# FFN gate and up by seven block products for eight, with GpSimd sums of weight blocks

## The chip, the cores and the metric

The kernel runs on one core of a Trainium2 chip. The metric is device time in microseconds (us), the median over runs. A profile of one execution gives, for every instruction, when it ran on its engine and what it waited for. The engines are TensorE (PE; PEld is its weight load), VectorE (DVE), ScalarE (ACT), GpSimd (POOL) and SyncE (SP, which here issues the transfers). PSUM is the memory that TensorE writes its products to, SBUF the other memory on the chip.

## The reference

Two layers of a decoder trunk on 512 tokens with 1024 channels, in float32. Only the second half of a layer is changed, the gated feed-forward network (FFN):

```
h2 = rms_norm(x, g_ffn[l])                                  # x * 1/sqrt(mean(x*x) + eps) * g
gt = causal_dwconv(h2 @ w_ffn_gate[l], ffn_conv_w[l])       # 3 taps over tokens, by channel
x = x + (jax.nn.silu(gt) * (h2 @ w_ffn_up[l])) @ w_ffn_down[l]
```

The weights w_ffn_gate and w_ffn_up are 1024 x 2816 each, w_ffn_down is 2816 x 1024. The four mixing branches ahead of the FFN are left alone.

## The kernel before

Activations lie with channels on the 128 partitions and 512 tokens along a row. A float32 product is made of three passes: each operand is split into its rounding to float32r (hi) and the rest (lo), and hi*hi, hi*lo and lo*hi are added up in one PSUM bank. So every matmul has a 128x128 block of weights as its stationary operand and 512 tokens as the moving one, and three of them do one block of the product.

Weights come by SP in units of 512 KB (tile `raw`, four blocks of 128 rows by 256 columns), in the order of a list (`plan`). `split_weights` makes a unit's pair: ScalarE writes `hi` (line 283), VectorE writes `lo` as the difference (line 284). There are three buffers each of `hi` and `lo`, so the split of a unit starts when the unit three ahead of it in the list has been multiplied. `channels` multiplies two units for a pair of output tiles, and `tick` lets queued jobs emit work amid a unit. PE and VectorE run in the order in which the code is written; so does ScalarE by the program as built.

`feed` makes the operand of the FFN: for each of x's eight channel tiles k, `xh` and `xl` (lines 178, 179) and the sum of squares (lines 186, 187). The factor 1/sqrt(...) of the norm by token is not known yet when the first product begins. It is made by the job "rows": `columns` (four one-column matmuls over the summed squares, a root and a reciprocal), then `spread` (four transposes), which leaves it in `rows`.

`ffn` goes through the 22 tiles of 128 hidden channels in three parts (`PARTS`: 8, 8 and 6 tiles). In a part it takes two tiles at a time (a pair): gate's product (96 matmuls for gate and up together), times `rows` (line 981), the three taps (983, 986) and Silu (989) on VectorE and ScalarE; then up's product, the gate value times `rows` (994), times up (995), and its split into hi and lo (169, 170). Then `down` multiplies the part's tiles by w_ffn_down and adds the result to x (1006). In the last layer's last part down gives tokens on partitions, and `store` writes the output.

Of the kernel before, what the change touches and what calls it, by code (L numbers as in the profile page):

```python
# [23 lines left out]
P = 128  # L24
# [20 lines left out]
def turn_pieces(n=6, bits=11):  # L45
    """1 / (2 pi) as a sum of numbers of few bits."""
    from fractions import Fraction
    pi = Fraction(3141592653589793238462643383279502884197169399375105820974944592307816406286,
                  10 ** 75)
    rest, out = 1 / (2 * pi), []  # L50
    for _ in range(n):
        e = math.floor(math.log2(float(rest)))
        unit = Fraction(2) ** (e - bits + 1)
        piece = (rest // unit) * unit
        out.append(float(piece))
        rest -= piece
    return out
# [3 lines left out]
def trunk(ctx: ExitStack, tc, x, positions, g_mix, w_in, b_gate, g_qa, g_ka, g_kidx, w_oa,  # L61
# [18 lines left out]
    def b_tile():  # L80
        return tmp.tile([P, 542], F32, tag="b", name=nm("b"), bufs=6)

    def m5_tile(w=1280):
        return tmp.tile([P, w], F32, tag="m5", name=nm("m5"), bufs=3)

    def h8_tile(shape):
        return tmp.tile(shape, F32, tag="h8", name=nm("h8"), bufs=3)
# [19 lines left out]
    # ---------------------------------------------------------------- inputs  # L107
# [8 lines left out]
    # ---------------------------------------------------------------- vectors by channel  # L116
    # Their rows, turned to a column each.
# [35 lines left out]
    # ---------------------------------------------------------------- residual stream  # L153
# [13 lines left out]
    def split(hi, lo, src):  # L167
        """hi: src rounded to float32r; lo: the remainder (in place where lo is src)."""
# [3 lines left out]
    def feed(k, gname, l):  # L172
        """x's tile k as an operand, times its gain, and its squares; kept in DRAM while the
        branches need its place."""
        if gname == "g_mix" and k % 4 == 3:
# [4 lines left out]
                                       op1=OP.subtract)  # L180
        if k == 0:
# [6 lines left out]

    def inv_root(acc, n, rows, sums=None):
        """1 / sqrt(sum over channels / n + eps): by token, and that for all partitions in rows.  # L190
        Three stages, and where the first will be. sums: by token, in four parts each."""
# [25 lines left out]
    # ---------------------------------------------------------------- weights  # L217
    # In units (source, first k, k's, columns), in the order in which they are used.
# [13 lines left out]
    def ffn_units(w, l, f):  # L232
        return [(w[l, h * 512:(h + 1) * 512, f * P:(f + 2) * P], 4 * h, 4, 256) for h in range(2)]

    def down_units(l, f0, f1, p):
        h = (f1 - f0) // 2
        return [(w_ffn_down[l, (f0 + i * h) * P:(f0 + (i + 1) * h) * P, p * 256:(p + 1) * 256],
                 i * h, h, 256) for i in range(2)]

    def plan():  # L240
        for l in range(L):
# [20 lines left out]
            for f0, f1 in PARTS:  # L262
                for f in range(f0, f1, 2):
                    yield from ffn_units(w_ffn_gate, l, f)
                    yield from ffn_units(w_ffn_up, l, f)
                for p in range(4):
                    yield from down_units(l, f0, f1, p)

    def unit(tag, dtype, nk, w):
        t = wts.tile([P, UNIT], dtype, tag=tag, name=nm(tag), bufs=3)  # L270
        return t[:, :nk * w].rearrange("p (k n) -> p k n", k=nk)

    def fetch(src, nk, w):
        """[128 nk, w] of a matrix on chip, [128, nk, w]."""
        raw = unit("raw", F32, nk, w)
        nc.sync.dma_start(raw, src.rearrange("(k p) n -> p k n", p=P))  # L276
        return raw

    def split_weights(raw, nk, w, step):
        """The same as a pair of operands."""  # L280
# [9 lines left out]
    def fetch_next():  # L290
        u = stream.popleft()
        near.append((u, fetch(u[0], u[2], u[3])))

    def ahead(n, step=4):
        while len(ready) < n and (near or stream):
# [3 lines left out]
            ready.append((u, split_weights(raw, u[2], u[3], min(step, u[2]))))  # L299

    def weights(src, k0, nk, w):
        """The next pair of the plan; two more are under way."""
# [5 lines left out]
    # Work beside the products: jobs of stages, (cost on VectorE, what it does) each. A stage that  # L308
    # needs TensorE comes a tick after what it waits for.
# [16 lines left out]
    # late: the rest of a stage, once the others of its tick have begun.  # L326
# [85 lines left out]
    # ---------------------------------------------------------------- constants  # L412
# [9 lines left out]
    def make_constants():  # L422
        # [t, s]: 0 where s <= t, NEG elsewhere, in the last 128 columns.
# [3 lines left out]
        # [t, s]: 0 where s < t, NEG elsewhere.  # L427
# [19 lines left out]
    def make_angles(pos_i):  # L447
        """Cosines and sines of positions times frequencies; the rest of it as jobs."""
# [10 lines left out]
        def products():  # L459
# [8 lines left out]
            # The angle in turns: both factors in parts whose products are exact.  # L468
# [35 lines left out]
    def rope(v, nh, half, t, f0):  # L504
        """Rotates v [128 tokens, nh, width] by the angles of token tile t."""
# [13 lines left out]
    # ---------------------------------------------------------------- one layer's mixing  # L519
    def mixing(l, first):  # L520
# [5 lines left out]
        # Indexer queries, keys and weights, and the values, from x times gain; the norm after.  # L526
# [4 lines left out]
        def normed(ks):  # L531
            """The normed x takes the place of x times gain."""
# [32 lines left out]
        # --- indexer  # L565
# [62 lines left out]
        # --- attention queries and keys  # L628
# [25 lines left out]
        # --- selected attention, a head and 128 tokens at a time  # L654
# [69 lines left out]
        # --- conformer branch  # L724
        u, conv, yb = [], [], []

        def conv_taps(c, j0, j1):
            if j0 == 0:
                a = b_tile()
                nc.vector.tensor_scalar(a[:, :T], u[c][:, :T], col(f"cb_w{l}", c),  # L730
                                        col("cb_b", l * 4 + c), op0=OP.mult, op1=OP.add)
                conv.append(a)
# [55 lines left out]
        for p in range(2):  # L788
# [6 lines left out]
            ps = channels(in_units(l, O_GLU + 256 * p, 256), xop, 256)  # L795
            for c in range(2):
                a = b_tile()
# [14 lines left out]
        # --- short convolution branch  # L812
# [33 lines left out]
        def merge(n, y):  # L846
            """Adds a branch to the merged sum: its gate times its output projection."""
# [33 lines left out]
        # --- stick-breaking attention, keys in rows  # L881
# [16 lines left out]
        def stick(h, t):  # L898
# [3 lines left out]
            def weigh():  # L902
                """A key's weight: its break times the product of what later keys have kept."""
# [54 lines left out]
        for p in range(4):  # L958
            ps = channels(merge_units(l, p), merged, 256)
            for c in range(2):  # L960
                k = 2 * p + c
                nc.vector.tensor_tensor(xT[k], xT[k], ps[c], op=OP.add)
                feed(k, "g_ffn", l)

    # ---------------------------------------------------------------- one layer's FFN
    def ffn(l, last):
        done.clear()
        rows = act.tile([P, T], F32, tag="rows", name=nm("rows"), bufs=1)
        _, columns, invert, spread = inv_root(lambda: norm["acc"][:, :T], D, rows)
        job(0, "rows", [], PAUSE, (0.1, lambda: (columns(), invert())), (0.1, spread))  # L970
        budget[0], credit[0] = 0.1, 0.0
        for f0, f1 in PARTS:
            ops = []
            for f in range(f0, f1, 2):
                ps = channels(ffn_units(w_ffn_gate, l, f), xop, 256)
                need("rows")
                sl = []
                for c in range(2):
                    g = s_tile()
# [164 lines left out]
```

## Time and profile before

| | us |
|---|---|
| median of the timed runs | 1990.86 (1990.49 to 1990.98, 3 runs) |
| span of the profiled execution, first to last instruction | 1989.1 |
| PE busy in it | 1977.1 |
| DVE busy | 1314.1 |
| ACT busy | 777.7 |
| POOL busy | 11.8 |

The profiled execution has its span as its own time; the timed runs lie 1.8 us above it, which is what lies around the span. Busy times count an engine's running instructions; an engine that waits is idle. The granted clock is the share of TensorE's full clock of 2.4 GHz.

### The profile page before, as it was taken

How to read it: one execution, taken by the hardware profiler on the slowest of the kernel's cores; microseconds unless marked ns; L12 is line 12 of the kernel's file. 1: busy time of each engine (PE TensorE's matmuls, PEld its weight loads, DVE VectorE, ACT ScalarE, POOL GpSimd, SP SyncE). 2: the span in 40 equal slices, each digit the busy share in tenths (PEclk: the TensorE clock that was granted, in tenths of full speed). 3: DMA queues.
4: the chain of work that ended last, by engine and by line, in shares of the span. 5: the costliest groups of instructions: out<-in, count | busy, mean ns of one | idle time of the engine just before them, and what ended most of it. 6: DMA issues, size and time to landing. Idle time of an engine off the chain costs nothing.

```text
span 1989.1 us, 23980 instructions
## 1 busy us (share of the span) xinstructions
PE 1977.1 (99%) x9244; PEld 1642.2 (83%) x9244; DVE 1314.1 (66%) x2208; ACT 777.7 (39%) x1266; POOL 11.8 (1%) x129
## 2 busy tenths in 40 slices
PE   8999999999999999999999999999999999999999
PEld 7878888888888888888888888888888888888888
DVE  7887789767445654646667878896764556456364
ACT  6436442443634322222353464424444343223231
POOL 0000000000000000000000000000000000000000
PEclk9999999999999999999999999999999999999999
DMA  6333223233333333333342332232333323333322
GB/s 198 96 96 85 66 84 96 85 107 95 96 96 96 95 97 95 106 96 93 104 127 85 87 94 75 75 104 75 110 94 96 96 85 106 101 91 105 95 85 86
DMA packets 176440, 191.46 MB, mean 96 GB/s; under 512 B 6310, under 2 KB 167110, under 8 KB 175302
## 3 DMA queue, kind: packets, MB, share of 16 engines
q1 hardware_dynamic: 176326, 189.93, 31.8%
q8 instruction: 73, 1.20, 0.3%
q14 instruction: 41, 0.34, 0.1%
HBM read 183.62 MB, written 6.29 MB: 95 GB/s over the span
## 4 chain that ended last, share of the span: by engine, by line
PE 98%; DMA 1%; SPq 0%; ACT 0%; DVE 0%; issue 0%; ACTq 0%
PE mm L105 92%; PE at L105 4%; PE at L685 0%; PE at L927 0%; DMA x<-in_x_dram 0%; DMA raw<-in_w_in_dram 0%; PE at L650 0%; PE at L1022 0%; ACT hi L283 0%; SPq L435 0%; PE at L211 0%; PE at L589 0%; ACT L672 0%; SPq L125 0%; SPq L276 0%
## 5 line engine op out<-in xcount | busy, mean ns | idle before, releaser
L283 ACT ACTIVATE hi<-raw 128x1024 fp32r<-128x1024 f32 (+3 forms) x344 | 358.8, 1044 | 777.1 <-PE mm L105 730.2
L105 PE MATMUL mm<-xh,hi 128*128 128x512 f32 x1664 | 656.6, 395 | 0.0
L105 PE MATMUL mm<-xh,lo 128*128 128x512 f32 x1664 | 648.4, 390 | 0.0
L105 PE MATMUL mm<-xl,hi 128*128 128x512 f32 x1664 | 648.0, 389 | 0.0
L284 DVE TENSOR_TENSOR lo<-raw,hi 128x1024 fp32r<-128x1024 f32 (+2 forms) x342 | 412.2, 1206 | 320.1 <-ACT hi L283 320.1
L105 PE MATMUL mm<-q,hi 128*128 128x512 f32 x1248 | 396.9, 391 | 0.0
L105 PEld LDWEIGHTS mm<-xh,hi 128*128 128x128 f32 x1664 | 312.6, 188 | 67.9 <-issue 2.8
L105 PEld LDWEIGHTS mm<-xh,lo 128*128 128x128 f32 x1664 | 312.5, 188 | 65.5
L105 PEld LDWEIGHTS mm<-xl,hi 128*128 128x128 f32 x1664 | 312.7, 188 | 65.0 <-issue 1.0
L105 PEld LDWEIGHTS mm<-q,hi 128*128 128x128 f32 x1248 | 233.5, 188 | 49.8 <-issue 2.1
L105 PE MATMUL mm<-q,lo 128*128 128x512 f32 x688 | 268.0, 389 | 0.0
L736 DVE SCALAR_TENSOR_TENSOR b<-b,par,b 128x512 f32<-128x512 f32 x240 | 180.2, 751 | 6.9
L105 PEld LDWEIGHTS mm<-q,lo 128*128 128x128 f32 x688 | 129.2, 188 | 26.8
L105 PE MATMUL mm<-hi,xh 128*128 128x512 f32 (+1 forms) x320 | 120.3, 382 | 1.4 <-ACT hi L283 1.1
L105 PE MATMUL mm<-lo,xh 128*128 128x512 f32 (+1 forms) x320 | 117.9, 374 | 0.0
L105 PE MATMUL mm<-hi,xl 128*128 128x512 f32 (+1 forms) x320 | 117.9, 374 | 0.0
L169 ACT ACTIVATE q<-s 128x512 fp32r<-128x512 f32 x68 | 43.0, 632 | 98.6 <-DVE s L995 62.8
L105 PEld LDWEIGHTS mm<-hi,xh 128*128 128x128 f32 x320 | 60.6, 191 | 13.9 <-issue 1.9
L986 DVE SCALAR_TENSOR_TENSOR s<-s,par,s 128x512 f32<-128x512 f32 x88 | 66.2, 752 | 6.5 <-DVE s L983 0.5
L105 PEld LDWEIGHTS mm<-hi,xl 128*128 128x128 f32 x320 | 59.6, 188 | 10.1
L105 PEld LDWEIGHTS mm<-lo,xh 128*128 128x128 f32 x320 | 59.6, 188 | 9.7
L170 DVE TENSOR_TENSOR q<-s,q 128x512 fp32r<-128x512 f32 x52 | 36.0, 693 | 37.5 <-ACT q L169 37.5
(199 smaller groups left out, 1570.6 us busy)
## 6 DMA issues: line engine op xcount, KB each, us to landing
raw<-in_w_in_dram SPq DMA_DIRECT2D x152, 512.0 KB, 3.6
raw<-in_w_ffn_gate_dram SPq DMA_DIRECT2D x44, 512.0 KB, 3.7
raw<-in_w_ffn_up_dram SPq DMA_DIRECT2D x44, 512.0 KB
raw<-in_w_ffn_down_dram SPq DMA_DIRECT2D x32, 512.0 KB, 3.3
raw<-in_w_merge_dram SPq DMA_DIRECT2D x16, 512.0 KB, 4.0
raw<-in_w_ffn_down_dram SPq DMA_DIRECT2D x16, 384.0 KB, 2.9
away<-h SPq DMA_DIRECT2D x4, 1024.0 KB, 5.9
raw<-in_w_oc_dram SPq DMA_DIRECT2D x8, 512.0 KB, 3.4
```

The source lines that it names most:

```text
L105: return nc.tensor.matmul(*a, skip_group_check=True, **k)
L169: nc.scalar.activation(hi, src, AF.Copy)
L170: nc.vector.tensor_tensor(lo, src, hi.bitcast(F32), op=OP.subtract)
L283: nc.scalar.activation(hi[:, k:k + step], raw[:, k:k + step], AF.Copy)
L284: nc.vector.tensor_tensor(lo, raw, hi.bitcast(F32), op=OP.subtract)
L736: nc.vector.scalar_tensor_tensor(a[:, :T], u[c][:, j:j + T], col(f"cb_w{l}", j * 4 + c), a[:, :T], op0=OP.mult, op1=OP.add)
L986: nc.vector.scalar_tensor_tensor(a[:, :T], g[:, j:j + T], col(f"f_w{l}", 22 * j + f + c), a[:, :T], op0=OP.mult, op1=OP.add)
```

## The change

Gate and up of a pair form a matrix of 2 x 2 blocks: two halves of the input channels by (gate, up). With the tokens cut in two halves of H = 256, the product of such a pair takes eight block products, and Strassen's scheme (in Winograd's form) does it in seven, with sums of blocks of the weights and of the activations. A product is one `step`: 24 matmuls of 256 tokens, 168 for a pair.

* The sums of weight blocks are four GpSimd instructions over 128 x 1024 for each pair (`add` in `block`): s1 = up0 + up1, s2 = s1 + gate0, s3 = s2 - up1 (written over gate0), s4 = s2 + gate1. Each is then split by ScalarE and VectorE as a unit was.
* The sums of activation blocks are made by `feed_ffn`, in place of `feed`, once a layer.
* The sums of products are made in PSUM: a bank is copied (`after_g1`), or written by VectorE (`join`), and PE adds further products onto it.
* The norm's factor is no longer applied to the hidden values of up, but to down's result (lines 1217 and 1223); the first tap's product goes from VectorE to ScalarE, the small memset from GpSimd to VectorE.
* `quad_order` gives the order of the steps: g1 of the next pair comes ahead of s3, s4 and u2 of a pair; in a part's last pair the order is s1, s2, g2, s3, s4, u2.

```diff
+    def feed_ffn(k, l):
...
+        j = k - 4
+        e1, e2, d, d4 = s_tile(), s_tile(), s_tile(), s_tile()
+        nc.scalar.activation(e2[:, :T], xT[k], AF.Copy, scale=g)
+        nc.scalar.activation(e1[:, :T], xT[j], AF.Copy, scale=col("g_ffn", l * KD + j))
+        nc.scalar.activation(xh[k], xT[k], AF.Copy, scale=g)
+        t3, n2, t4 = d[:, :H], d[:, H:T], d4[:, :H]
+        nc.vector.tensor_tensor(t3, e2[:, H:T], e1[:, H:T], op=OP.subtract)
+        nc.vector.scalar_tensor_tensor(n2, t3, -1.0, e1[:, :H], op0=OP.mult, op1=OP.subtract)
+        nc.vector.scalar_tensor_tensor(t4, n2, -1.0, e2[:, :H], op0=OP.mult, op1=OP.subtract)
+        nc.vector.tensor_tensor(xl[k], e2[:, :T], xh[k].bitcast(F32), op=OP.subtract)
...
+        split(*both, d[:, :T])
+        split(*four, t4)
...
+        squared(k)
...
+    def quad_order(f0, f1):
+
+        yield f0, ("g1",)
+        for f in range(f0, f1, 2):
+            if f + 2 < f1:
+                yield f, ("s1", "g2", "s2")
+                yield f + 2, ("g1",)
+                yield f, ("s3", "s4", "u2")
+            else:
+                yield f, ("s1", "s2", "g2", "s3", "s4", "u2")
...
+        def add(to, x, what, op=OP.add):
+            nc.gpsimd.tensor_tensor(b[to], b[x], b[what], op=op)
...
+        if step == "s1":
+            load("s", w_ffn_up, 0, "raw", wts)
+            load("u2", w_ffn_up, 1, "b", tmp)
+            load("g2", w_ffn_gate, 1, "b", tmp)
+            add("s", "s", "u2")
+            return b["s"]
+        if step == "s2":
+            add("s", "s", "g1")
+            add("g1", "s", "u2", OP.subtract)
+            return b["s"]
+        if step == "s4":
+            add("s", "s", "g2")
+            return b["s"]
...
+    def product(l, f, step, bank, fresh):
+
+        hi, lo = block_weights(l, f, step)
+        for c in range(2):
+            dst = bank[:, c * H:(c + 1) * H]
+            for k in range(4):
+                oh, ol = comb[BLOCK_OF[step], k]
+                w = slice(c * P, (c + 1) * P)
+                mm(dst, hi[:, k, w], oh, start=fresh and c == k == 0, stop=False)
+                mm(dst, hi[:, k, w], ol, start=False, stop=False)
+                mm(dst, lo[:, k, w], oh, start=False, stop=k == 3)
+            if c == 0:
+                tick(budget[0])
...
+            def join():
+                v["z"] = ps_mm()
+                nc.vector.tensor_tensor(v["z"], v["v"], v["u"][:, :T], op=OP.add)
...
+                    product(l, f, step, bank, step in ("g1", "s1"))
+                    for g in after.get(step, ()):
+                        g()
+                    if pending and step in ("s1", "s2", "g2"):
+                        pending.popleft()()
+                    if step == "s3" and f + 2 >= f1:
+                        first_half()
+                        join()
```

First place: VectorE's queue from one pair to the next. Before, this stands there for gate and up of one pair (`lo` rows are splits of weights, `rows` the norm's factor, `q` an operand of down):

```order
L284 TENSOR_TENSOR lo_6319<-raw_6317,hi_6320 128x1024
L994 TENSOR_TENSOR s_6272<-s_6272,rows_5336 128x512
L995 TENSOR_TENSOR s_6272<-mm_6285,s_6272 128x512
L170 TENSOR_TENSOR q_1089_6349<-s_6272,q_1089_6349 128x512
L994 TENSOR_TENSOR s_6280<-s_6280,rows_5336 128x512
L995 TENSOR_TENSOR s_6280<-mm_6286,s_6280 128x512
L170 TENSOR_TENSOR q_1090_6354<-s_6280,q_1090_6354 128x512
L284 TENSOR_TENSOR lo_6361<-raw_6359,hi_6362 128x1024
```

In the changed kernel this stands there at a part's last pair, from the second half of the pair ahead (line 1148) to the `join` (line 1135) of the last; its s4 adds onto the bank that `join` writes. The splits in it are g2 (`b_7367`), s3 (`raw_7223`), s4 (`raw_7363`) and u2 (`b_7365`):

```order
L1148 TENSOR_TENSOR s_7294<-mm_7331,rows_5410 128x256
L394 TENSOR_TENSOR lo_7436<-b_7367,hi_7437 128x1024
L1157 SCALAR_TENSOR_TENSOR s_7429<-s_7293,par,s_7429 128x512 x2
L1157 SCALAR_TENSOR_TENSOR s_7430<-s_7294,par,s_7430 128x512 x2
L394 TENSOR_TENSOR lo_7470<-raw_7223,hi_7471 128x1024
L1166 TENSOR_TENSOR s_7429<-mm_7082,s_7429 128x256
...
L176 TENSOR_TENSOR q_1230_7507<-s_7430,q_1230_7507 128x512
L394 TENSOR_TENSOR lo_7511<-raw_7363,hi_7512 128x1024
L394 TENSOR_TENSOR lo_7539<-b_7365,hi_7540 128x1024
L1130 TENSOR_TENSOR s_7569<-at_7299,rows_5410 128x256
...
L1135 TENSOR_TENSOR mm_7575<-at_7435,s_7498 128x512
```

Between two uses of the same kind there are now seven splits for four, and the taps and the product of the pair ahead stand in front of the `join` on which PE waits.

Second place: PE at the start of a layer's FFN, where the sum of squares (`s` behind `ones`) is taken to a column. Before, 36 matmuls of 512 tokens of the first gate product stand between the merge and it (the last four are shown, `xh` and `xl` being the activations):

```order
L105 MATMUL mm_5338<-xh_93,lo_5296 128x512
L105 MATMUL mm_5338<-xh_94,hi_5297 128x512
L105 MATMUL mm_5338<-xl_102,hi_5297 128x512
L105 MATMUL mm_5338<-xh_94,lo_5296 128x512
L105 MATMUL at_5388<-ones,s_5106 128x1 x4
```

Now 36 matmuls of 256 tokens stand there, 24 of step g1 and 12 of s1 (whose last four are shown):

```order
L111 MATMUL at_5443<-xh_89,lo_5344 128x256
L111 MATMUL at_5443<-xh_90,hi_5345 128x256
L111 MATMUL at_5443<-xl_98,hi_5345 128x256
L111 MATMUL at_5443<-xh_90,lo_5344 128x256
L111 MATMUL at_5462<-ones,s_5111 128x1 x4
```

The four one-column matmuls come after as many matmuls as before, each of half the tokens.

Third place: VectorE at the same point, the last of x's eight tiles. Before, for tiles 6 and 7 (`h` is x, `s_5106` the sum of squares):

```order
L962 TENSOR_TENSOR h_757_4132<-h_757_4132,mm_5262 128x512
L179 SCALAR_TENSOR_TENSOR xl_101<-h_757_4132,par,xh_93 128x512
L187 TENSOR_TENSOR s_5106<-s_5106,s_5327 128x512
L962 TENSOR_TENSOR h_757_4132<-h_757_4132,mm_5263 128x512
L179 SCALAR_TENSOR_TENSOR xl_102<-h_757_4132,par,xh_94 128x512
L187 TENSOR_TENSOR s_5106<-s_5106,s_5333 128x512
```

Now, for tile 7 alone, `s_5394` and `s_5395` being its sums of activation blocks, behind the same eight rows of tile 6:

```order
L1081 TENSOR_TENSOR h_753_4129<-h_753_4129,mm_5306 128x512
L238 TENSOR_TENSOR s_5394<-s_5393,s_5392 128x256
L239 SCALAR_TENSOR_TENSOR s_5394<-s_5394,s_5392 128x256
L240 SCALAR_TENSOR_TENSOR s_5395<-s_5394,s_5393 128x256
L241 TENSOR_TENSOR xl_102<-s_5393,xh_94 128x512
L176 TENSOR_TENSOR m_911_5103<-s_5394,m_911_5103 128x512
L176 TENSOR_TENSOR spare<-s_5395,m_912_5104 128x256
L196 TENSOR_TENSOR s_5111<-s_5111,s_5407 128x512
```

Three instructions a tile have become eight, and the last of them, the addition to the sum of squares, is what `columns` reads. GpSimd's queue holds the four sums of a pair in place of two memsets of two columns, 88 in all, with s1 of the next pair ahead of s4 of a pair.

## Rows read from the trace of the kernel before

**Rows 1.** The page: span, busy times, and PE's granted clock by slice.

```profile
span 1989.1 us, 23980 instructions
...
PE 1977.1 (99%) x9244; PEld 1642.2 (83%) x9244; DVE 1314.1 (66%) x2208; ACT 777.7 (39%) x1266; POOL 11.8 (1%) x129
...
PEclk9999999999999999999999999999999999999999
```

**Rows 2.** The longest of PE's waits: us in total, times, longest.

```profile
PE at L1089 <- POOL nones L432: 2.4, 1, 2.4
```

**Rows 3.** Window of one pair: length, then busy by engine, clock, DMA share, GB/s.

```profile
1812.87:1834.63 21.76, 21.76 (x97) 18.02 (x96) 13.97 (x19) 6.66 (x8) 0.20 (x2) 1.00 0.32 102
```

**Rows 4.** PE's timeline in the last down product: start, duration, instruction.

```profile
1939.77 0.39 PE L105 MATMUL mm<-xh,hi 128*128 128x512 f32 x1
...
1951.10 0.39 PE L105 MATMUL mm<-xh,lo 128*128 128x512 f32 x1
```

**Rows 5.** Tile q: shortest/mean/longest ns, first to last start, shape, count.

```profile
L105 PE MATMUL mm<-hi,q x192: 277/283/284, 1951.3 to 1985.8; 128*128 128x256 f32 x192
...
L105 PE MATMUL mm<-lo,q x96: 282/283/284, 1951.4 to 1985.6; 128*128 128x256 f32 x96
```

**Rows 6.** VectorE's timeline in that pair; in brackets the wait ahead.

```profile
1812.87 1.23 DVE L284 TENSOR_TENSOR lo<-raw,hi 128x1024 fp32r<-128x1024 f32 x1 [2.31 <-ACT hi L283]
1814.01 0.68 DVE L994 TENSOR_TENSOR s<-s,rows 128x512 f32<-128x512 f32 x1
1814.80 0.69 DVE L995 TENSOR_TENSOR s<-mm,s 128x512 f32<-128x512 f32 x1
1816.19 0.69 DVE L170 TENSOR_TENSOR q<-s,q 128x512 fp32r<-128x512 f32 x1 [0.70 <-ACT q L169]
1816.80 0.69 DVE L994 TENSOR_TENSOR s<-s,rows 128x512 f32<-128x512 f32 x1
...
1826.87 1.54 DVE L986 SCALAR_TENSOR_TENSOR s<-s,par,s 128x512 f32<-128x512 f32 x2
1828.33 0.68 DVE L981 TENSOR_TENSOR s<-mm,rows 128x512 f32<-128x512 f32 x1
```

**Rows 7.** ScalarE's groups by form: busy, mean ns; idle time ahead.

```profile
L283 ACT ACTIVATE hi<-raw 128x1024 fp32r<-128x1024 f32 x320 | 339.6, 1061 | 739.5 <-PE mm L105 696.9 <-issue 32.3 <-ACT s L186 3.4
...
L989 ACT ACTIVATE s<-s 128x512 f32<-128x512 f32 x44 | 27.5, 626 | 37.4 <-DVE s L986 37.4
...
L178 ACT ACTIVATE xh<-h,par 128x512 fp32r<-128x512 f32 x24 | 17.2, 718 | 31.0 <-DVE h L962 20.5 <-DVE h L1006 10.6
```

**Rows 8.** VectorE's groups by form, of constants, transposes and sums.

```profile
L1032 DVE TENSOR_TENSOR m<-m,mm 128x256 f32<-128x256 f32 x8 | 3.4, 421 | 8.3 <-PE mm L105 8.3
...
L1084 DVE COPY h<-at 128x512 f32<-128x512 f32 x4 | 2.6, 679 | 0.0
...
L482 DVE TENSOR_TENSOR m<-m,m 128x1152 f32<-128x1152 f32 x1 | 1.4, 1359 | 0.0
...
L480 DVE TENSOR_SCALAR m<-m 128x1152 f32<-128x1152 f32 x1 | 0.8, 752 | 0.0
```

**Rows 9.** PE's timeline at the start of the first layer's FFN.

```profile
637.36 0.39 PE L105 MATMUL mm<-xh,hi 128*128 128x512 f32 x1
...
645.52 0.95 PE L105 MATMUL at<-ones,s 128*128 128x1 f32 x8
```

**Rows 10.** VectorE's timeline at the same place.

```profile
634.84 0.69 DVE L962 TENSOR_TENSOR h<-h,mm 128x512 f32<-128x512 f32 x1 [0.58 <-PE mm L105]
...
639.76 0.69 DVE L187 TENSOR_TENSOR s<-s,s 128x512 f32<-128x512 f32 x1
```

**Rows 11.** GpSimd's groups by form.

```profile
masks.py:199 POOL TENSOR_SCALAR_AFFINE_SELECT ident<-ident 128x128 f32<-128x128 f32 x1 | 0.3, 292 | 0.0
...
masks.py:197 POOL MEMSET ident<- 128x128 f32 x1 | 0.2, 204 | 0.3 <-POOLq L1130 0.3
...
L112 POOL MEMSET eps<- 128x1 f32 x1 | 0.1, 98 | 0.0
```

More of the change, by code (lines that the diff above doesn't have):

```diff
@@ L187, in feed, with pieces @@
             nc.vector.tensor_tensor(norm["acc"][:, :T], norm["acc"][:, :T], sq[:, :T], op=OP.add)
+    H = T // 2
+    comb, spare = {}, const.tile([P, H], F32R, name="spare")
+    pairs, singles = [], []
+    def pieces():
+        m = [h8_tile([P, 4 * T], F32R)] + [m5_tile(5 * H, F32R) for _ in range(3)]
+        pairs[:] = [m[0][:, i * T:(i + 1) * T] for i in range(4)]
+        pairs.extend(a[:, i * T:(i + 1) * T] for a in m[1:] for i in range(2))
+        singles[:] = [a[:, 4 * H:] for a in m[1:]] + [spare]
+        for i in (8, 9):
+            singles.extend(pairs[i][:, c:c + H] for c in (0, H))
@@ L305, in weights, with block_weights @@
         assert (u[0].tensor.name, u[0].offset, u[1:]) == (src.tensor.name, src.offset, (k0, nk, w))
+        return pair
+    def block_weights(l, f, step):
+        ahead(depth[0])
+        u, pair = ready.popleft()
+        assert u == (l, f, step), (u, l, f, step)
         return pair
@@ L996, in ffn @@
                     q = q4_tile()
-                    split(q[:, 0], q[:, 1], a)
-                    ops.append((q[:, 0], q[:, 1]))
+                    split(q[:, 0], q[:, 1], a[:, :T])
+                    ops[f + c] = (q[:, 0], q[:, 1])
+            return v, {"g1": (after_g1,), "s2": (after_s2,), "s3": (after_s3,), "s4": (up_half,)}, \
+                first_half, join, (second_half, taps, multiply)
+        for part, (f0, f1) in enumerate(PARTS):
+            state, pending = {}, deque()
+            for f, steps in quad_order(f0, f1):
+                if f not in state:
+                    state[f] = quad(f)
+                v, after, first_half, join, rest = state[f]
+                for step in steps:
+                    if step == "g1":
+                        v["f"] = ps_at()
+                    elif step == "s1":
+                        v["v"] = ps_at()
+                    bank = v[{"g1": "f", "g2": "f", "s1": "v", "s4": "z"}.get(step, "y")]
+                    product(l, f, step, bank, step in ("g1", "s1"))
[6 more added lines that the diff above has]
+                        join()
+                    if step == "s2" and f + 2 < f1:
+                        first_half()
+                if steps == ("g1",) and f > f0:
+                    state[f - 2][3]()
+                if steps[-1] == "u2":
+                    rest[0]()
+                    pending.extend(rest[1:])
+            while pending:
+                pending.popleft()()
+            some = [ops[f] for f in range(f0, f1)]
@@ L1008, in ffn @@
                         feed(k, "g_mix", l + 1)
-                    elif last and f1 == PARTS[-1][0]:
-                        job(0, f"out{k}", [], PAUSE, (0.1, lambda k=k: turn_out(k)))
     outs = []
     def turn_out(k):
-        if k == 0:
-            h = h8_tile([P, 2, NT, 256])
-            outs.extend([h[:, 0], h[:, 1]])
-            outs.extend(m5_tile(2 * T).rearrange("p (t c) -> p t c", t=NT) for _ in range(2))
         ps = ps_at()
```

189 lines of the change are left out of this document (136 added, 53 removed).

## The prediction

> **What bounds the kernel now.** I read the page first [rows 1]: PE is busy for 1977.1 of 1989.1 us and its granted clock is full in all forty slices, so next to nothing but matmuls sets the end. PE's waits come next: the longest of all is 2.4 us, once [rows 2]. So fewer columns through PE are worth their whole time, and every new wait of PE costs its whole time. The window of one pair, from one gate to the next, shows what room the others have [rows 3]: 21.76 us, all of it PE's, with 13.97 of VectorE, 6.66 of ScalarE and 0.20 of GpSimd. VectorE is the engine to watch, since the change gives it more splits.
>
> The timed median lies 1.8 us above the profiled span of 1989.1. The sum is made for the span, and 1.8 is added at the end.
>
> **PE's part.** A matmul's own duration contains its pipeline, so I take the distance of starts. From the first to the last of [rows 4] 50 matmuls of 512 tokens take 11.33 us, 0.2266 each; a pair is 96 of them, 21.75 us, the window. The 288 matmuls of 256 columns in [rows 5] start over 34.5 us, 0.1202 each, each with a new stationary block, as the changed kernel's will. A pair becomes 168 x 0.1202 = 20.19 us: 1.57 less, **-34.5 us** for 22 pairs. The saving is gone if the distance is 0.1295.
>
> The Trainium skill ("TensorE: Matmul & The Clock Gate", section on the back-to-back issue gap) allows 518 cycles for 512 columns and 262 for 256. By that a pair would go from 20.7 to 18.3 us and the change would save 52 us, and the time below would be 2052. The rows are longer at both widths, so I give it no chance of its own.
>
> **VectorE's and ScalarE's prices.** From starts in [rows 6]: a split of a unit 1.14, an operation over 512 tokens 0.61, 0.79 where the next one needs its result, two taps of a tile 1.46, and 0.70 for each wait on ScalarE's half of an operand. ScalarE takes 1.06 for a unit's hi, 0.63 for 512 tokens without and 0.72 with a scale by channel [rows 7]. A 256-column operation is 0.42 [rows 8], some 0.35 back to back. After the change a pair asks of VectorE seven splits (8.0), `first_half` 0.8, `join` 0.6, `up_half` 0.6, `second_half` 0.7, taps 2.9 and `multiply` 4.2 with its two ScalarE waits: 17.8 us of PE's 20.2. ScalarE has about 13. As averages both fit; what PE waits for depends on the order, so I follow the chains at the places of the order rows.
>
> **Start of a layer's FFN, twice.** Before, PE reaches `columns` 36 matmuls or 8.16 us after the first gate matmul [rows 9], and the sum of squares was ready at 639.76 + 0.69, 3.1 us after it [rows 9, 10]. Now those 36 matmuls take 4.3 us, and the sum comes later. With t = 0 at the first gate matmul: x's tile 6 is summed by -1.8 (634.84 + 0.69 [rows 10]), ScalarE's three scaled copies last until 0.2; its next instruction is the hi of s2, which waits for the buffer of g1 (ended at 3.05) and ends at 4.1; only then come tile 6's splits (till 5.7), square and sum (6.3). Tile 7 is added to x by 7.0, its three copies last till 9.0, the three sums of blocks on VectorE till 9.8, xl 10.4, splits 11.4, the sum of squares 12.0. PE stands from 4.3 to 12.0: 7.7 us, **+15.4** for both layers.
>
> **From pair to pair, 10 times.** There are three buffers of hi and lo, so the splits of g2 wait until s4 of the pair ahead is multiplied. From there (t = 0), ScalarE's and VectorE's queues being in order: hi of g2 1.06, its lo 2.2, `second_half` 2.9, two scaled copies on ScalarE and the hi of s2 5.1, its lo 6.2, taps 9.1, lo of the next g1 10.3, `multiply` 14.4, lo of s3 15.6; then PE has some 22 matmuls of s3 and 24 of s4 left (5.5) and 0.28 until the last completes. The loop is 21.4 us long against PE's 20.2: 1.2 each, **+12**.
>
> **The last pair of a part, 6 times.** Here s4 adds onto the bank that `join` writes, and all of the pair ahead stands before `join` in VectorE's queue. t = 0 is again the end of s4. GpSimd's sum for s2 can start when the lo of s1 has been read out (-0.4) and ends at 2.1 (price below); hi 3.2, lo 4.3, `second_half` 5.0, lo of g2 6.1, taps 9.0, lo of s3 10.2, `multiply` 14.6, lo of s4 15.8, of u2 16.9, `first_half` 17.7, `join` 18.4. PE has five steps of 24 matmuls until then, 14.4 us: 4.05 each, **+24**.
>
> **Down's start.** After u2 PE goes on to down, whose operands of the last pair need `second_half`, the copies, taps, Silu, and half of `multiply`: 7.0 us. In a part of 8 tiles down reaches them after 6.8 us (30 matmuls of 0.2266), in one of 6 after 4.8 (21): 0.25 four times and 2.3 twice, **+5.6**. The factor on down's result is VectorE's beside PE. At the very end 128-column operations in twos replace one of 256: +0.3.
>
> So far the span changes by -34.5 + 15.4 + 12 + 24 + 5.6 + 0.3 = **+23**, with GpSimd beside VectorE for nothing.
>
> **GpSimd's sums.** No row shows one. GpSimd fills 128 columns in 204 ns and one in 98, 0.83 ns a column; with one read it takes 292, 1.53 [rows 11]. One read more would make 2.23 ns, and 0.1 + 1024 x 2.23 = 2.4 us for a sum, the value I take; 1.7, if the second read is free, is the lower end, and 3.2 (a read each at the whole price) the upper. Four a pair fill 9.5 of 20.2 us.
>
> **Do they hinder VectorE?** VectorE goes through 1152 columns of SBUF in 752 ns with one operand and in 1359 with two, and reads 512 from PSUM in 679 [rows 8]: two operands in SBUF cost it double, as though each stream had one way in and a single operand both. No row shows GpSimd reading meanwhile; it is all but idle. If it reads through one of the two ways, the splits, the taps and the operands' lo (13 of VectorE's 17.8 us) and the sums exclude each other: 13 + 9.5 = 22.5 us, over PE's 20.2 even if packed without a gap. In the loop about two of the four sums fall amid VectorE's chain from g2 to s3 and push it back by their length, 2 x 2.4; the others lie in waits on ScalarE. That is 10 x 4.8 = 48; in a last pair one sum and a third, 6 x 3.2 = 19. Ends: 0, and 67 (with 3.2 us a sum 90). I take 56, since gaps of 0.7 and more at ScalarE's round trips let parts of a sum through.
>
> The Trainium skill ("SBUF — State Buffer", section "Who interferes with whom") states this case: a VectorE instruction with two SBUF inputs contends with a GpSimd one that reads SBUF, and whoever issues second blocks until the first ends. No run here shows it; it speaks against this change.
>
> The sum: +23 + 56 = +79, a span of 2068 and a time of **2070 us**.
>
> **Rivals.**
> A, GpSimd hinders nobody: 1990.9 + 23 = 2014 us. For it: VectorE's double price for two operands may be a limit inside it. Against: see above. Chance 0.25.
> B, the other side: VectorE's chain of a pair stays inside PE's time. My chains add up serial steps; if hi and lo of one unit overlap others by 1.2 us more in a loop and 4 us more in a last pair, and sums do not hinder, PE waits only at the two starts and down's: -34.5 + 15.4 + 5.6 = -13.5, 1977 us. It decides at chains 6% and 22% shorter. For it: 17.8 is below 20.2. Against: PE's order of steps leaves `join` no slack. Chance 0.09.
> C, the half-width matmuls do not run in half the time between other sources: from 0.1295 on the change saves nothing, +34.5 on the forecast, 2105 us. Against: [rows 5] are 288 of them with loads. Chance 0.04.
>
> **How the numbers follow.** The forecast with sums that hinder has 0.59, with 2045 to 2100 as its own range; the remaining 0.03 is chains that come out near no change. The range, 1995 to 2100, leaves out B, C and the ends. What a measurement of this kernel tells from no change is about 0.2% (4 us). Faster is B: 0.09; same 0.03; slower 0.88.
>
> **What would show it.** Right: PE's starts 0.120 apart in 256-token steps; a PE wait of 7 to 8 us ahead of the one-column matmuls on `ones`; PE waits on VectorE's `join` in six places; GpSimd's sums at 2.2 us or above; and VectorE's lo splits of 1024 columns, now 1.22 us [rows 6], longer wherever a sum runs. Wrong: lo splits that stay at 1.22 beside running sums (then A); PE's waits under 1% with sums of 1.7 us (then B); starts 0.13 apart (then C). If the clock falls in the long waits, PE loses more than I say; no row shows a wait long enough to price that.

## The result, and the profile after

The changed kernel takes 2112.5 us (median of 4 runs, 2110.6 to 2118.1) against 1990.7: 1.062 times as long, interval 1.060 to 1.063. The forecast of 2070 us (1995 to 2100) had the direction, by its own mechanism, and was 42 us short. The page of the changed kernel (span, busy times, granted clock by slice):

```profile
span 2108.8 us, 27803 instructions
...
PE 1994.6 (95%) x10828; PEld 1727.9 (82%) x10828; DVE 1506.0 (71%) x2459; ACT 929.9 (44%) x1498; POOL 234.7 (11%) x173
...
PEclk9999999999998999999999999999999989999999
```

Beside [rows 1], PE is no longer busy throughout, and its granted clock is below full in two of the slices. Two views say where the time is. PE's waits (line and what it waited for: us in total, times, longest), where [rows 2] had 2.4 us as the longest:

```profile
PE at L111 <- DVE lo L394: 32.6, 17, 2.9
PE at L111 <- DVE s L196: 21.1, 3, 10.3
PE mm L111 <- DVE mm L1135: 20.1, 6, 3.8
PE mm L111 <- ACT s L1122: 12.6, 6, 2.1
PE mm L111 <- DVE lo L394: 12.3, 9, 2.0
```

All of PE's waits sum to 110.5 us, before the change to 8.9. The view of the core (span, mean granted clock):

```profile
core 0: 2108.8 us, clock 0.975
```

A mean clock of 0.975 over 2108.8 us is a loss of 52.7 us, but what of it fell while PE stood is in the waits already. The clock was at 0.50 in twenty stretches; their sum, with PE's busy time in them:

```profile
sum 105.83, PE 85.08 PEld 84.40 DVE 64.13 ACT 36.88 POOL 4.85; mean PE 4.25 PEld 4.22 DVE 3.21 ACT 1.84 POOL 0.24
```

PE was busy for 85.1 us of them, so the clock cost half of that, 42.5 us, beside the waits. A third term is small: a wait is counted from the end of the last matmul, 0.28 us after its start, while in a stream the next one starts after 0.12, so each wait costs 0.16 us more than it shows; 57 waits for 12 before make 7 us. The account is -34.5 for the shorter products + (110.5 - 8.9) + 42.5 + 7 = +117, and the span is 119.7 longer; 3 us stay open.

**What one wait looks like.** From one pair to the next in the first layer, VectorE's timeline and then GpSimd's:

```profile
678.65 3.10 DVE L394 TENSOR_TENSOR lo<-raw,hi 128x1024 fp32r<-128x1024 f32 x1 [2.02 <-ACT hi L393]
681.67 5.02 DVE L1157 SCALAR_TENSOR_TENSOR s<-s,par,s 128x512 f32<-128x512 f32 x4
686.60 1.22 DVE L394 TENSOR_TENSOR lo<-raw,hi 128x1024 fp32r<-128x1024 f32 x1
```

```profile
674.95 5.71 POOL L366 TENSOR_TENSOR raw<-raw,b 128x1024 f32<-128x1024 f32 x2
681.88 2.81 POOL L366 TENSOR_TENSOR raw<-raw,b 128x1024 f32<-128x1024 f32 x1 [1.22 <-DVE lo L394]
```

The first lo starts while GpSimd is in the second of two sums and ends 1.1 us after that sum does (680.66): it took 3.10 us for 1.22. Four taps take 5.02 us, twice the 1.46 of a pair in [rows 6] and 2.1 more, with a sum amid them. The split behind the taps, with GpSimd idle, takes 1.22 again, but it starts late. It is the lo of the next pair's g1, and PE waits for it (PE's timeline, then the windows before, in, behind and well behind the wait, with the columns of [rows 3]):

```profile
684.54 0.28 PE L111 MATMUL at<-xh,hi 128*128 128x256 f32 x1
684.66 0.28 PE L111 MATMUL at<-xl,hi 128*128 128x256 f32 x1
687.88 0.58 PE L111 MATMUL at<-xh,lo 128*128 128x256 f32 x1 [2.94 <-DVE lo L394]
688.26 0.41 PE L111 MATMUL at<-xh,hi 128*128 128x256 f32 x1
688.47 0.41 PE L111 MATMUL at<-xl,hi 128*128 128x256 f32 x1
```

```profile
683.00:684.60 1.60, 1.60 (x16) 1.60 (x15) 1.60 (x1) 0.00 (x0) 1.60 (x1) 1.00 0.00 0
684.70:687.80 3.10, 0.23 (x2) 0.03 (x1) 3.06 (x5) 1.71 (x3) 0.00 (x0) 0.89 0.57 160
687.90:692.70 4.80, 4.80 (x22) 4.80 (x23) 3.29 (x7) 3.09 (x5) 0.00 (x0) 0.50 0.01 4
694.00:696.00 2.00, 2.00 (x19) 2.00 (x18) 2.00 (x3) 0.31 (x1) 0.00 (x0) 1.00 0.76 211
```

Ahead of the wait starts are 0.12 us apart and the granted clock is full. Behind 2.94 us of standing it is 0.50, the lower of the two levels (1.2 GHz), starts are 0.21 apart, and it stays so for some 6 us in which PE is busy without a gap: the wait cost 2.9 us and about as much again.

Not every long wait does. Behind another of 2.94 us, which ended at 978.46, the clock is full:

```profile
978.50:981.50 3.00, 3.00 (x23) 2.86 (x24) 1.93 (x5) 2.29 (x4) 0.00 (x0) 1.00 0.02 7
```

Of the 28 waits of 2 us and more ahead of VectorE's and ScalarE's results, eight have no half clock within 4 us behind them; each of these is followed within 8 us by another wait that has. What decides it the runs do not show.

**Which VectorE instructions are slowed.** Groups by form in the same trace (VectorE, then GpSimd; mean ns is the number behind the busy time). Line 1216 reads one operand from PSUM (`mm`), line 1217 behind it two from SBUF, on the same 512 columns (without sums line 1217 takes 692 ns); line 1157 is the taps:

```profile
L1157 DVE SCALAR_TENSOR_TENSOR s<-s,par,s 128x512 f32<-128x512 f32 x88 | 84.4, 980 | 4.3 <-ACT s L1150 2.8
...
L394 DVE TENSOR_TENSOR lo<-b,hi 128x1024 fp32r<-128x1024 f32 x44 | 73.1, 1662 | 24.9 <-ACT hi L393 24.9
...
L1217 DVE TENSOR_TENSOR mf<-mf,rows 128x512 f32<-128x512 f32 x16 | 18.4, 1147 | 0.5
...
L1216 DVE TENSOR_TENSOR mf<-mm,mf 128x512 f32<-128x512 f32 x16 | 11.0, 688 | 6.9 <-PE mm L111 6.9
```

```profile
L366 POOL TENSOR_TENSOR raw<-raw,raw 128x1024 f32<-128x1024 f32 x22 | 52.8, 2400 | 242.2 <-issue 147.1 <-DVE lo L394 95.1
```

A sum that nothing delays takes 2.40 us, the value that the prediction took from [rows 11].

### The profile page after: what moved, and what is told of

It is laid out like the page before. It is cut to its first block, busy times and chain, and to the rows that moved or that the text cites. A ratio compares the mean times of both kernels' runs of the same rounds, so it can differ in the third digit from the quotient of the medians.

```text
span 2108.8 us, 27803 instructions
## 1 busy us (share of the span) xinstructions
PE 1994.6 (95%) x10828; PEld 1727.9 (82%) x10828; DVE 1506.0 (71%) x2459; ACT 929.9 (44%) x1498; POOL 234.7 (11%) x173
## 5 line engine op out<-in xcount | busy, mean ns | idle before, releaser
L111 PE MATMUL mm<-xh,hi 128*128 128x512 f32 (+1 forms) x1136 | 438.0, 386 | 20.1 <-DVE mm L1135 20.1
L111 PE MATMUL mm<-xh,lo 128*128 128x512 f32 (+1 forms) x1136 | 429.3, 378 | 0.0
L111 PE MATMUL mm<-xl,hi 128*128 128x512 f32 (+1 forms) x1136 | 428.9, 378 | 0.0
L111 PEld LDWEIGHTS mm<-xh,hi 128*128 128x128 f32 x1136 | 219.6, 193 | 62.2 <-DVE mm L1135 21.5
L366 POOL TENSOR_TENSOR raw<-raw,b 128x1024 f32<-128x1024 f32 x66 | 174.5, 2651 | 676.1 <-DVE s L196 385.0
L111 PE MATMUL at<-xh,lo 128*128 128x256 f32 x528 | 157.5, 298 | 32.6 <-DVE lo L394 32.6
L111 PE MATMUL at<-xh,hi 128*128 128x256 f32 x528 | 155.8, 295 | 0.0
L111 PE MATMUL at<-xl,hi 128*128 128x256 f32 x528 | 155.1, 294 | 0.0
L111 PEld LDWEIGHTS at<-xh,lo 128*128 128x128 f32 x528 | 107.4, 203 | 36.1 <-DVE lo L394 36.1
L111 PE MATMUL mm<-m,hi 128*128 128x256 f32 x660 | 130.8, 289 | 0.0
```

The costliest lines, as they stand in the source:

```text
L111: return nc.tensor.matmul(*a, skip_group_check=True, **k)
L366: nc.gpsimd.tensor_tensor(b[to], b[x], b[what], op=op)
```

## The experiments

Theory 1: a GpSimd sum and a VectorE instruction with both operands in SBUF shut each other out, and PE's long waits bring stretches at half clock behind them. Rivals: the order of VectorE's work alone makes the waits (2), or the sums cost as late links of a chain (2a); the clock falls because the short matmuls follow each other faster (3). Times are medians; the kernel before ran beside each at 1989.9 to 1990.2 us.

### The sums left out, and sums replaced by writing

```diff
-            nc.gpsimd.tensor_tensor(b[to], b[x], b[what], op=op)
+            pass
```

> The changed kernel with GpSimd's 88 sums left out (a step multiplies the block as it was loaded, so the output is not the reference's). Theory 1: a sum and a VectorE instruction with both operands in SBUF shut each other out for whole instructions, and every PE wait of 2 us and more is followed by a stretch at half the granted clock. Then lo of 128x1024 is back to 1.22 us everywhere and the taps to 0.75, PE's waits fall from 111 us to about 40, what the clock takes falls from about 54 us to about 20: 1990 - 34.5 + 28 + 20 = about 2005 us (1985 to 2035). Rival 2: VectorE's order of work alone makes the waits, sums or not: above 2080 us. Rival 3: the clock falls because 256-token matmuls follow each other faster, waits or not: granted clock stays near 0.975.

```diff
-            nc.gpsimd.tensor_tensor(b[to], b[x], b[what], op=op)
+            nc.gpsimd.memset(b[to], 0.02)
+            nc.gpsimd.memset(b[to], 0.02)
+            nc.gpsimd.memset(b[to][:, :2], 0.02)
```

> The changed kernel with each GpSimd sum replaced by three GpSimd fills of the same tile (1024, 1024 and 512 columns, about 2.4 us as a sum takes), which wait for the same things and are waited for by the same, but read nothing (so the output is not the reference's). Theory 1 (shared reading): VectorE's lo back to 1.22 us although GpSimd is as busy, time within 15 us of the run without sums, about 2015 us. Rival 2a (the sums cost as links of the chain, through when they end): time stays within 15 us of 2112 us.

Without sums 2034.6 us (ratio 1.022, 1.020 to 1.024); with writing in their place 2035.5 (1.023, 1.021 to 1.024). GpSimd is nearly as busy as with the sums (219.8 us for 234.7), its writing stands in the same places of the chain, and VectorE is undisturbed (groups by form of the run with writing; GpSimd, then VectorE):

```profile
L366 POOL MEMSET raw<- 128x1024 f32 x88 | 84.4, 959 | 855.2 <-DVE s L196 385.1 <-DMA raw<-in_w_ffn_up_dram 263.6 <-DVE lo L396 187.4
```

```profile
L396 DVE TENSOR_TENSOR lo<-b,hi 128x1024 fp32r<-128x1024 f32 x44 | 53.7, 1221 | 24.8 <-ACT hi L395 24.8
...
L1159 DVE SCALAR_TENSOR_TENSOR s<-s,par,s 128x512 f32<-128x512 f32 x88 | 64.1, 749 | 4.3 <-ACT s L1152 2.8
```

So 77 us of the 122 are GpSimd's reading beside VectorE, not its time nor its place in the chain: rival 2a is out, and rival 2 with its 2080 us. What is left, 45 us over before, is the order's. I had expected 2005 us for the run without sums, with some 40 us of waits and 20 of clock; the waits that remain were 61.5 us and the clock's cost while PE was busy 20.5 (the mean clock is 0.987). PE's waits of the run without sums:

```profile
PE mm L111 <- DVE mm L1135: 22.6, 6, 4.0
PE at L111 <- DVE s L196: 16.0, 3, 7.4
PE mm L111 <- DVE lo L394: 10.4, 11, 1.1
```

At the place shown above the four taps now take 2.98 us for 5.02, the lo of the next pair's g1 is in time, and PE waits for the lo of s3 behind it instead, 1.0 us (VectorE's timeline, then PE's):

```profile
675.41 2.98 DVE L1157 SCALAR_TENSOR_TENSOR s<-s,par,s 128x512 f32<-128x512 f32 x4
```

```profile
684.96 0.39 PE L111 MATMUL mm<-h,lo 128*128 128x256 f32 x1 [1.01 <-DVE lo L394]
```

The waits for join are no longer with the sums (20.1 us) than without (22.6). What the sums added in a part's last pair lies ahead of join, in PE's waits for ScalarE's copy (line 1122, 12.6 us; none without sums).

Against rival 3: the matmuls are as short here as in the changed kernel, and the clock came back with the waits, from 0.975 to 0.987.

### The taps' operands out of SBUF

The taps' sums go to two PSUM banks; up's second half stays in PSUM as well (not shown).

```diff
-                v["a"] = [s_tile() for _ in range(2)]
+                v["a"] = [v["z"], ps_at()]
...
-                    nc.scalar.activation(a, a, AF.Silu)
+                    v["a"][c] = s_tile()
+                    nc.scalar.activation(v["a"][c][:, :T], a, AF.Silu)
```

> The changed kernel with the taps' sums kept in PSUM (in the bank of the joined gate half and one more), Silu writing SBUF, and up's second half kept in PSUM: the taps and the products then read one operand from SBUF and one from PSUM. Sums and splits stay as they are. Theory 1: taps stay at about 0.75 us each beside a sum; the work that shuts GpSimd out falls from 13 to about 9.4 us a pair, 9.4 + 9.6 = 19 fits under 20.2; PE's waits fall to about 60 us and the time to about 2050 us (2030 to 2080). If GpSimd hinders any VectorE instruction: taps as long as before and 2112 us.

2102.5 us (ratio 1.056, 1.054 to 1.058), far from the 2050 that I expected. The taps are untouched by the sums now (753 ns for 980), while the splits, which still read twice from SBUF, are as slow as before. Groups by form:

```profile
L394 DVE TENSOR_TENSOR lo<-b,hi 128x1024 fp32r<-128x1024 f32 x44 | 73.1, 1660 | 24.7 <-ACT hi L393 24.7
...
L1159 DVE SCALAR_TENSOR_TENSOR at<-s,par,at 128x512 f32<-128x512 f32 x44 | 33.1, 753 | 0.8
```

The place of the operands decides, as theory 1 has it. The expected 60 us did not come, only 10: PE's waits for lo went from 44.9 to 18.4 us, those for ScalarE's copy of a bank (line 1122) from 12.6 to 21.2 and for join from 20.1 to 23.9. A link was shortened and the next one was late.

### Work for PE in place of its waits

In a step's product, and 80 times ahead of the columns at a layer's start (not shown):

```diff
+                for _ in range(n0 if c == k == 0 else n1 if c == 1 and k == 3 else 0):
+                    mm(dst, zero_diag[:, :P], zero_diag[:, :H], start=False, stop=False)
```

> The changed kernel with PE given products of zeros (bfloat16, 256 columns) to do where it waited: 80 ahead of the columns at a layer's start, 24 amid g1 of a pair that follows another, 17 at the end of g2 and 31 at the end of s3 in a part's last pair; they add zero to the sums. All waits of the others stay as they are. Theory 1 (clock falls after PE has stood): granted clock back to about 1.0 and the time down by most of the 54 us, to about 2065 us (2055 to 2085), the products of zeros costing about what the waits did. Rival 3 (clock falls from the rate of the short matmuls): clock 0.975 or lower, 2105 us or more.

2117.7 us (ratio 1.064, 1.063 to 1.066): the time did not fall, and the reason is mine: 832 products of zeros were more than PE had waited. Its waits went down by 63.5 us, to 47.0, while the products kept it busy for 96.0 (groups by form):

```profile
L111 PE MATMUL at<-zero_diag 128*128 128x256 bf16 x646 | 74.7, 273 | 0.0
...
L111 PE MATMUL mm<-zero_diag 128*128 128x256 bf16 x186 | 21.3, 273 | 0.0
```

The clock is what the run was for:

```profile
core 0: 2117.2 us, clock 0.991
```

With PE busy through more than half of its waits, the clock's cost while it is busy falls from 42.5 to 18.7 us, though more matmuls of 256 columns ran: rival 3 is out a second time. That a filled wait makes the kernel faster is not shown by this run.

### Sums by transfers

```diff
-            nc.gpsimd.tensor_tensor(b[to], b[x], b[what], op=op)
+            src = b[what] if op == OP.add else rows_of(ffn_block(w_ffn_up, l, 0, f))
+            nc.gpsimd.dma_start(b[to], src, accum_op=OP.add)
```

> The changed kernel with its sums of weight blocks made by accumulating transfers that GpSimd issues (s3 as gate0 + up0, from DRAM) in place of GpSimd additions; all else as it was, and the result is the reference's. Theory 1: no engine's instruction reads SBUF beside VectorE, so lo is back to 1.22 us and the time is that of the run without sums, 2035 us, if a transfer lands within some 4 us: 2030 to 2050. Rival: transfers that are late or share the queues with the weights take the place of the hindrance, 2060 us or more with waits on lo.

2104.1 us (ratio 1.057, 1.056 to 1.059). The hindrance is gone (lo 1220 ns), and the transfers are late in its place. DMA issues (KB each, median us from issue to landing), and PE's waits:

```profile
raw<-b POOLq DMA_DIRECT2D x44, 512.0 KB, 6.0
```

```profile
PE mm L111 <- DVE mm L1136: 43.0, 6, 7.9
```

Half of the sums, which took 2.4 us, land after 6.0, and in a part's last pair, where s1 and s2 follow each other, join is up to 7.9 us late. Theory 1 on the hindrance stands; the rival on the transfers is what set the time.

### Order alone, and order with transfers

`hi_first` puts the 16 products by hi of a step ahead of the 8 by lo:

```diff
+        for half in range(2):
+            for c in range(2):
...
+                    if half:
+                        mm(dst, lo[:, k, w], oh, start=False, stop=k == 3)
+                        continue
```

> The changed kernel with the 16 products by hi of a step ahead of its 8 products by lo, so that lo may come 1.7 us later; GpSimd's additions stay. If the waits are links that end last (45 us of PE's waits are for lo): those fall to a few us, with their part of the clock, to about 2060 us. Rival: VectorE with the hindrance has more than 20.2 us of work a pair, so the slack is eaten within a few pairs and the wait goes to another link (join, the copies on ScalarE): 2095 to 2112 us.

2092.7 us (ratio 1.052, 1.050 to 1.053). The rival's number: waits for lo fell from 44.9 to 9.5 us, those for ScalarE's copy rose to 29.2 and for join to 26.1.

With join ahead of `multiply` as well:

```diff
-                    if step == "s3" and f + 2 >= f1:
+                    if step == ("g2" if f + 2 >= f1 else "s2"):
                         first_half()
                         join()
```

> hi_first, and the join of a pair right behind its first half, ahead of the product of the pair before (multiply), which moves behind the next g1 or s3. GpSimd's additions stay. Theory 1: the six waits on join (20 us and their clock) go, VectorE and GpSimd together still need more than PE: 2050 to 2085 us. If the order alone was the trouble (rival 2): below 2000 us.

2087.0 us (ratio 1.049, 1.047 to 1.051), just above what I gave. The waits on join went, as expected, and 22.5 us of waits for lo came in their place; I take it that the sums keep VectorE over PE's time in whatever order (13 + 9.6 us a pair for 20.2, an estimate). And with transfers, a layer's first g2 by input tile, and a later place for the columns (two more `PAUSE` in the job "rows"):

> The three together (accumulating transfers, hi first, join ahead of multiply), and at a layer's start the columns two steps later and the first g2 by input tile. With nothing beside VectorE, 17.8 us of its work under PE's 20.2, and join with slack, only the layer's start (some 4 us twice), down's start (5.6) and a little clock are left: 1990 - 34.5 + 8 + 6 + 8 = about 1978 us (1965 to 1995), faster than both kernels.

2074.7 us (ratio 1.042, 1.041 to 1.044): 97 us worse than I expected. ScalarE stood in its queue for transfers that had not landed, and the copies behind it came late (19.9 us of PE's waits). ScalarE's waits:

```profile
ACT hi L394 <- DMA raw<-raw: 58.5, 18, 8.2
```

### Two sums by transfer, two by GpSimd, and link after link

s1 and s3 have time and become transfers; s2 and s4 stand in the chain and stay with GpSimd; the taps in PSUM, and both orders from above:

```diff
-            add("s", "s", "u2")
+            nc.gpsimd.dma_start(b["s"], b["u2"], accum_op=OP.add)
```

> hi first and join ahead of multiply, with s1 and s3 (as gate0 + up0) made by accumulating transfers, which have time, and s2 and s4, which stand in a chain, by GpSimd; the taps' sums in PSUM. What shuts out is then 2 x 2.4 us of sums and some 10 of VectorE's, 15 of 20.2 us a pair. Theory 1: lo longer than 1.22 us in a few places only, waits of PE about 50 us (two layer starts 20, the rest 30), 2020 us (2000 to 2045). Rival: VectorE's and ScalarE's queues in order are bound by other links (the transfers, the copies), 2045 to 2075 us as in the runs before.

> mix2, and at a layer's start the next pair's g1 ahead of the first g2, x's last tile fed behind the split of that g2, and the columns amid s2. The two starts lose 20 us of waits and their clock against mix2 if the operand chain was what PE waited for: 20 to 28 us less than mix2; if the start waits move to another link, less than 8 us.

2038.9 us (ratio 1.025, 1.023 to 1.026) and 2037.0 (1.024, 1.022 to 1.025). mix2 is within its bounds, 74 us below the changed kernel with the same arithmetic, but the gain of mix3 failed: the start's 7 us became three shorter waits (2.3, 0.6 and 1.8 us in the first layer) with as much half clock behind them.

> mix3 with the links that its trace shows late taken out: s3's transfer right behind g1's split, and s2 made from its result (s3 + up1); a layer's last tile rounded to xh first; columns amid s2 and their spread amid s3 of the first pair; the last pair's second half ahead of u2; down's first product taking both output tiles by input tile in its second unit. mix3 stood for about 38 us more than before the change, in waits that each brought a stretch at half clock (about 71 us of it, 35 us lost). If those waits were all that is left: 1990 - 34.5 + 15 + 15 = about 1985 us, faster than before (1970 to 2005). If the waits move on to other links once more: 2010 to 2035 us.

2016.8 us (ratio 1.013, 1.012 to 1.015): at each start one wait of 2.4 us was left, and those for ScalarE's copy ahead of s3 grew from 18.0 to 24.2 us.

> mix4 with its last long waits taken out: in a part's last pair the taps of the pair ahead come behind s2 and behind the copy of the bank that s3 adds onto (six waits of 2.8 us there); in a layer's first pair that copy is VectorE's, s2's sum is an accumulating transfer (so nothing shuts out the lo of the next g1, which came 2.4 us late), and s4 is split behind it. mix4 had 24 + 4.8 us of such waits and about 45 us at half clock (22 us lost). If both go: 1990 - 34.5 + 8 + 8 = about 1973 us, faster than before (1965 to 1985). If the clock does not come back with the waits: 1985 to 1995.

1998.8 us (ratio 1.004, 1.003 to 1.006), outside both of the bounds that I gave. The waits for the copy went, but join took 8.6 us in six places, so that PE's waits fell only from 45.2 to 30.6 us; the mean clock rose from 0.989 to 0.993, so it did come back with them.

> mix6 with join ahead of the taps too in a part's last pair (six waits of 1.4 us there), and at a layer's start the adding of x's last tile and its three copies ahead of the split of g2 (waits of 1.9 and 0.6 us, with 3 to 14 us at half clock behind them). If the shorter products give their 34.5 us in full and only waits and clock take it back: 8.6 + 3 us of waits and some 8 us of clock less, about 1982 us (1975 to 1990), faster than before. If something else keeps it: 1993 us or more.

1999.5 us (ratio 1.004, 1.003 to 1.006), not the 1982 expected: join's waits were gone, and PE waited 12.8 us for the lo of down's first unit instead.

```diff
+            if late and not k0:
+                for i in (0, 1, 2):
...
+                        for k in range(nk) if i == 2 else ():
+                            mm(ps[c], lo[:, k, c * P:(c + 1) * P], ops[k][0], start=False,
+                               stop=False)
```

> mix7 with down's first unit of a part by its hi products first (and in the last part its second by input tile), since mix7's trace has PE waiting 2.1 us for that unit's lo in six places (14.8 us in all), with half clock behind some. If waits and their clock are all that keeps the 34.5 us back: 14 us of waits and some 5 of clock less than mix7, about 1981 us (1975 to 1988). If the wait goes to the operands of down's last tiles: 1990 to 1998.

1996.7 us (ratio 1.003, 1.002 to 1.005), the rival's number: the wait went on to the operands of down's last tiles. PE's waits and the core of this last version:

```profile
PE mm L111 <- ACT q L175: 11.4, 9, 3.2
PE mm L111 <- ACT s L1224: 4.9, 1, 4.9
```

```profile
core 0: 1997.1 us, clock 0.994
```

All its waits are 34.9 us in 34 places, and PE was busy for 21.2 us at half clock. By the account of above, -34.5 + 26.0 + 10.6 + 3.5 (0.16 for each of 22 waits more) is +5.6, and it stands 8.0 above the span before: some 2 us stay open, and the saving is there and is spent on waits and their clock. No version ran faster than the kernel before.

## Why the prediction was wrong, point by point

**PE's part** was right: 0.12 us between starts in the steps of 24 matmuls, which leaves nothing of rival C, and the accounts of the runs close with the full 34.5 us to within 3 (the changed kernel, the run without sums, the one with writing, the last version).

**The chains of the order** were right in place and in size. Without sums I had priced 57.3 us of waits (15.4 + 12 + 24 + 5.6 + 0.3); the run without sums has 61.5 - 8.9 = 52.6, and 4 more for the 0.16 of each wait. Singly: 7.4 us at a layer's start (7.7 in the prediction), 22.6 / 6 = 3.8 at join (4.05), 1.0 for the lo of s3, ten times (1.2, ten times), and at down's first tiles 3.1 in all (5.6).

**GpSimd's sums**, 2.4 us, measured 2.40. **That they hinder VectorE** was the step I gave 0.59, and it is shown: reading is what costs. Its price in waits was 56 us in the prediction; 110.5 - 61.5 = 49.0 measured. It came at other places in part: 34.5 us in waits for lo (the prediction's 48 from pair to pair), 10 in the last pairs, at the copy and not at join (19), 5 at the layers' starts (none). The rule of the Trainium skill ("SBUF — State Buffer", section "Who interferes with whom"), that a VectorE instruction with two SBUF inputs and a GpSimd one that reads SBUF block each other and one that only writes does not, agrees with each of these runs: 3.10 us for 1.22 beside a sum, 1.22 beside writing, 753 ns for the taps with one operand in PSUM.

**The step that failed** is the last sentence of the prediction: "If the clock falls in the long waits, PE loses more than I say; no row shows a wait long enough to price that." I left the term out of the sum, that is, priced it at nothing. It was 42.5 us while PE was busy, 20.5 of them behind the order's waits (the run without sums) and 22 more with those that the hindrance added. With it the sum is 2070 + 42.5 - 4.5 (waits of 101.6 measured and 7 for their ends, for 113.3 added up) = 2108 us, against 2110.6 for the profiled execution. It also belongs to rival A: 2014 + 20.5 = 2034.5, and the run without sums took 2034.6.

I had not drawn on the page that speaks of it. The Trainium skill ("TensorE: Matmul & The Clock Gate", Part 1: The HAM clock gate) says that PE's clock is set by how busy PE has been; the trace agrees, with 1.00 ahead of 2.94 us of standing and 0.50 behind it. A change that makes PE wait at all should have had that as a term; by these runs it lies between nothing (978.46) and the wait's own size once more (2.9 us of standing, some 3 us lost behind it).

**The range** failed for the same reason: its upper end, 2100, is rival A's 2014 and 86 us of hindrance, nearly the worst that I had priced (90), but no clock.

**Rival B** (no waits but at the starts and down's, 1977 us) is what the later versions tried for. In each of them a link was shortened and the next one was late. That this is so because between s4 of one pair and down's first tiles the splits, taps and products of two pairs follow one another on VectorE and ScalarE is my reading; whether another order reaches 1977 us stays open.

## What to carry to other kernels

An engine that bounds a kernel by being busy without a gap loses more than the gap when it is made to wait: here 101.6 us of new waits cost 42.5 more, and a single wait of 2 us and more up to twice its length. Give PE the work that does not depend on the late operand first. Before work goes to GpSimd because VectorE is full, count which VectorE instructions beside it read two operands from SBUF: that time and GpSimd's add up (an estimated 13 + 9.6 us against 20.2 here), and an operand in PSUM takes an instruction out of the count. A saving of 1.57 us in 21.76 is smaller than one late link, so the chain has to be laid out to the end before the arithmetic is halved.

## What the runs showed of the hardware

Behind a PE wait of 2.94 us the granted clock was 0.50 for some 6 us of uninterrupted matmuls, behind another as long it was 1.00; in the changed kernel the half clock cost 42.5 us, some 0.4 of what its waits took themselves. A VectorE subtraction with both operands in SBUF took 3.10 us for 1.22 where a GpSimd sum ran, and 1.22 beside GpSimd's writing; with one operand in PSUM the taps took 753 ns beside sums, for 980 with both in SBUF. GpSimd's addition over 128 x 1024 took 2.40 us alone, and filling the same columns 0.96 us. An accumulating transfer of 512 KB from SBUF to SBUF landed 6.0 us after its issue (44 of them, the median; 4.4 for 22 others), against 3.7 for a load of as much from DRAM.
